# Stick-breaking attention: the keys' remaining shares overwrite the logits in PSUM, and the running product reads them there

## The chip, the cores and the metric

The kernel runs on one core of one Trainium2 chip. The metric is the device time of one execution in microseconds; the figure for a kernel is the median over its runs. The traces are of one profiled execution.

## What is computed

The reference is one layer with two branches that share an input projection: a gated delta rule (a recurrence over chunks of tokens) and stick-breaking attention (8 heads, 64 channels a head, 2048 tokens). Only the attention is touched here. For every query the keys are visited from the latest to the earliest; each takes the share sigmoid(z) of what the later keys have left over.

```python
z = jnp.einsum('bhqd,bhkd->bhqk', q[:, :, q0:end], k[:, :, :end]) * scale
mask = kj < qi
log_keep = jnp.where(mask, jax.nn.log_sigmoid(-z), 0.0)
rest = lax.cumsum(log_keep, axis=3, reverse=True) - log_keep
a = jnp.where(mask, jnp.exp(jax.nn.log_sigmoid(z) + rest), 0.0)
outs.append(jnp.einsum('bhqk,bhkd->bhqd', a, v[:, :, :end]))
```

## The kernel before

The kernel works in stages. The first projects the tokens and prepares the recurrence. Then the attention runs as background work between the matrix products of the last projections (the blocks of the gates): a generator, `attention`, emits the attention's instructions, and the projection calls it after every three products. A clock that the program itself keeps (it adds a cost for each product) decides when a piece is due: `LT`, `LP` and `LZ` are the delays between a tile's logits, its transposes, its products with v, and the next tile. The order of TensorE's instructions is pinned to the order in which they are emitted (`pin`), so TensorE runs the same list whatever the other engines do. The other engines' lists come from a scheduler. After the attention come the recurrence, the up projections and the output projection.

A tile of the attention is 128 queries by 512 keys (128, 256, 384 or 512 on the diagonal), 320 tiles in all, four to a step: 224 of them are 512 wide. The names in the trace for one tile:

- `z`, a bank of PSUM: logits, two products on TensorE (PE). On a diagonal block VectorE (DVE) adds `future`, which masks later keys (L1058; 128 instructions).
- `r` in SBUF: sigmoid of minus the logit, what a key leaves over, written by ScalarE (ACT, L1061); then overwritten in place by VectorE's running product from right to left (the scan, L1065). Its second tensor operand is `zero`, one column broadcast. Column `w` takes the value that the scan starts from (L1064, a copy of one column).
- `s` in SBUF: sigmoid of the logit (ACT, L1062), then multiplied on GpSimd (POOL) by `r` shifted by one column (L1068). These are the weights.
- `carry`: the scan's last value, copied for the tile of earlier keys (DVE, L1067).
- `at`: PE's transposes of `s`, two tiles to a bank (L128); `hi` (ACT, L1083) and `lo` (DVE, L1084) split them into two parts; `av`: PE's products of these with `vt`, summed over all steps of a head in one bank. `att_end` (L1044 on ACT, L1045 on DVE) reads `av` when a head is done; the next head's first product starts another.

`z` has two banks, `at` two, `av` two, `pj` (the projection's sums) two: all eight banks of PSUM. `s` has six buffers, `r` four. `att_pools` and `att_tile` are the functions whose code changes.

Of the kernel before, what the change touches and what calls it, by code (L numbers as in the profile page):

```python
# [18 lines left out]
P = 128  # L19
# [9 lines left out]
SD = 64  # L29
# [8 lines left out]
class Block:  # L38
    """The layer in three stages; DRAM scratch carries what a stage leaves for a later one."""

# [63 lines left out]
    def params(self):  # L104
        """The small parameters."""
        nc, i = self.nc, self.i
        rows = self.a([P, P], "rows")
        nc.gpsimd.memset(rows, 0.0)
        for t, n in ((self.alog, "a_log"), (self.dtb, "dt_bias")):
            self.load(t, i[n].partition_broadcast(P).rearrange("p o n -> p (o n)"))  # L110
        self.load(rows[0:48], i["conv_w"].rearrange("o t (r p) -> (o t r) p", p=P))
        self.load(rows[48:64], i["b_gate"].rearrange("o (r p) -> (o r) p", p=P))
        for k, n in enumerate(("sb_q_gain", "sb_k_gain")):
            for r in range(2):
                self.load(self.gqk[SD * r:SD * r + SD, k:k + 1], i[n].rearrange("o d -> d o"))
        nc.vector.tensor_mul(self.gqk[:, 0:1], self.gqk[:, 0:1], self.gqk[:, 1:2])
        ps = self.pt.tile([P, P], F32, tag="tp", name="tp")
        self.tr(ps, rows, self.ident)
        nc.vector.tensor_copy(self.cols, ps[:, 0:HB])
# [10 lines left out]
    def pin(self, ins):  # L130
        """Keep the tensor engine in program order."""
        if self.chain and self.last is not None:
            self.tc.add_manual_dep(ins.ins, self.last, mybir.DependencyInfo(mybir.DependencyClass.NoSync, mybir.DependencyReason.DATA), reason="order")
        self.last = ins.ins.name if self.chain else None

    def load(self, *args):
        """A load whose queue keeps program order during the first tiles."""
        ins = self.nc.sync.dma_start(*args)
# [5 lines left out]
    def defer(self, steps, fn):  # L144
        """Emit fn after the matrix products of `steps` further steps."""
        self.pending.append((self.now + steps, fn))
# [9 lines left out]
    def advance(self, amount, limit=4.0):  # L156
        """Let the background work emit about `amount` us of the tensor engine's time, or what it has ready."""
        if self.back is None:
# [17 lines left out]
    def drain(self):  # L176
        """All that is left of the background work."""
        while self.back is not None:
            self.advance(1e9)
            self.clock += 0.2  # L180
# [12 lines left out]

    # ---------------------------------------------------------------- stage 1
    def stage1(self):
# [62 lines left out]
    def ready(self, g):  # L258
        """Have the recurrence done for tokens of the up projections' group g."""
        while self.stored < 2 * g + 2:  # L260
# [12 lines left out]
    def gap(self):  # L273
        """Background work between the products of a projection; the recurrence follows the attention."""
        self.advance(self.third)
# [57 lines left out]
    def rsq(self, pool, ssq, n, scale, eps, tag):  # L333
        """(ssq * scale + eps) ** -0.5 on n columns."""
        nc = self.nc
# [6 lines left out]
    def prep_x(self, first):  # L342
        """Normalised x, transposed to channels by tokens, in two parts that f32r products carry exactly."""
        nc = self.nc
# [39 lines left out]
    def mm_chan(self, w, j, tg, between=None):  # L384
        """Projection block [128 channels, 512 tokens]."""
        hi, lo = w
# [9 lines left out]
    def mm_tok(self, w, t, ps, n):  # L396
        """Projection block [128 tokens, n channels]."""
        hi, lo = w
# [30 lines left out]
    def decays(self):  # L429
# [13 lines left out]
        nc.scalar.activation(s2, ab, AF.Sigmoid)  # L443
        # e = exp(-|xa|) = s1 / s2, log1p(e) = 2 atanh(e / (2 + e)), e / (2 + e) = s1 / (2 s2 + s1)
        nc.vector.scalar_tensor_tensor(s2, s2, 2.0, s1, ALU.mult, ALU.add)
# [55 lines left out]
    def qkb_store(self, qn, dst, kind, u, tp):  # L501
        """To channels by tokens, q with both gains, in two parts that f32r products carry exactly."""
        nc = self.nc
# [30 lines left out]
    def conv(self, ps, b, halo):  # L534
        """Causal four-tap convolution of a block; the caller multiplies what it returns for SiLU."""
        nc = self.nc
# [35 lines left out]
    def qk_tok(self, kq, tg, h):  # L572
        """Norms of q and k, k by tokens, and the decay between a chunk's tokens."""
        nc, wk = self.nc, self.wk
# [93 lines left out]

    # gated delta rule: within a chunk of 128 tokens, inverses of the two diagonal blocks of 64
    def dn_solve(self):  # L670
        """Unit triangular inverses by substitution, one block to a partition.

        With b[x, i] = -m[i, x] for x < i, step j adds b[x, j] b[j, i] to b[x, i]."""
        nc, wk = self.nc, self.sv
# [37 lines left out]
    def dn_states(self):  # L712
# [9 lines left out]
        def store(most=0):  # L722
            """Emit what is due, and all but `most` of the rest when its time comes."""
            while tails:
# [54 lines left out]
    def dn_chunk(self, c, loads, st, mo):  # L779
        """One chunk of the recurrence; k and q come without their norms, which nk, nbr and rq carry."""  # L780
        nc = self.nc
# [26 lines left out]
        nc.vector.tensor_tensor(o, ps, o, ALU.add)  # L808
        # rms over a head's values; o carries neither q's norm nor dk ** -0.5 yet
        nc.gpsimd.tensor_tensor(o, o, self.bc(self.rq, c), ALU.mult)  # L810
# [19 lines left out]

    # ---------------------------------------------------------------- stage 2
    def stage2(self):
        """The up projections follow the recurrence; then the rest."""
        NO = S // OG
# [29 lines left out]
    def run_job(self, jobs):  # L864
        """A piece of the first job; the next one's loads run ahead of its end."""
        if jobs:
# [15 lines left out]
    def split(self, src, k, g):  # L882
        """[128, OG] from DRAM in two parts, one of two sets."""
        nc, op = self.nc, self.op
# [17 lines left out]
    def up(self, g):  # L902
        """Gated sum of both up projections for OG tokens, channels by tokens."""
        nc = self.nc
# [34 lines left out]
    def att_pools(self, ctx):  # L939
        nc = self.nc  # L940
        self.ap = ap = ctx.enter_context(self.pool("ap", side="right"))
        self.pz = ctx.enter_context(self.pool("pz", bufs=2, space=PSUM, side="right"))
        self.pa = ctx.enter_context(self.pool("pa", bufs=2, space=PSUM, side="right"))
        self.pv = ctx.enter_context(self.pool("pv", bufs=2, space=PSUM, side="right"))
        self.one = ap.tile([P, 1], F32, name="one", bufs=1)
        self.zero = ap.tile([P, 1], F32, name="zero", bufs=1)
        nc.vector.memset(self.one, 1.0)
        nc.vector.memset(self.zero, 0.0)
        # added to a logit, it makes the key weigh nothing and break nothing
        self.future = ap.tile([P, P], F32, name="future", bufs=1)  # L950
        nc.vector.memset(self.future, -(2.0 ** 100))
        nc.gpsimd.affine_select(self.future, self.future, pattern=[[1, P]], compare_op=ALU.is_ge, fill=0.0, base=0, channel_multiplier=-1)

    # from a tile's products to its transposes, from there to the products with v, between two tiles, in us
    LT, LP, LZ = 4.5, 2.2, 1.3

    def attention(self):
        """Stick-breaking attention: one slot is a tile of 128 queries by 512 keys (or fewer on the diagonal)."""
        nc, ap = self.nc, self.ap
# [4 lines left out]
        def ready():  # L964
            """Emit what is due; the sets of buffers bound how far one kind runs ahead of another."""
            if prods and prods[0][0] <= self.clock:
# [84 lines left out]

    def att_tile(self, qt, kt, i, w, diag, carry):
        nc, ap = self.nc, self.ap
        z = self.pz.tile([P, TG], F32, tag="z", name="z")
# [5 lines left out]
        r = ap.tile([P, TG + 1], F32, tag="r", name="r", bufs=self.NR)  # L1060
        nc.scalar.activation(r[:, :w], z[:, :w], AF.Sigmoid, scale=-(SD ** -0.5))  # L1061
        nc.scalar.activation(s[:, :w], z[:, :w], AF.Sigmoid, scale=SD ** -0.5)  # L1062
        init = self.one if diag else carry[i]
        nc.vector.tensor_copy(r[:, w:w + 1], init)  # L1064
        nc.vector.tensor_tensor_scan(r[:, 0:w][:, ::-1], r[:, 0:w][:, ::-1], self.zero.to_broadcast([P, w]), init, ALU.mult, ALU.add)  # L1065
        carry[i] = ap.tile([P, 1], F32, tag=f"carry{i}", name="carry", bufs=2)
# [4 lines left out]
    def att_trans(self, A, m, edge):  # L1071
        """Two tiles' weights for two blocks of keys, the later block first, keys by queries in two parts."""
        nc, ap = self.nc, self.ap
# [43 lines left out]
```

## Time and profile before

| | us |
|---|---|
| median of 3 runs | 2150.53 |
| lowest and highest of them | 2144.36, 2152.09 |
| the profiled execution: span from first to last instruction | 2144.5 |
| PE busy in it | 2058.2 (96%) |
| DVE, POOL, ACT busy | 1493.9 (70%), 969.8 (45%), 875.2 (41%) |

For the profiled execution the profile gives the span and no other time. The shares are averages over stages with different limits; the attention lies between 794 us and 1589 us of the span, and what an edit to it is worth is read there. PE's matmuls are pipelined, so one that is shown to last 0.39 us may be followed by the next 0.23 us after its start.

### The profile page before, as it was taken

The numbers are of one execution on the slowest core, as the hardware profiler recorded it, in microseconds if no ns is written. First come the engines' busy times: TensorE is split into PE (matmuls) and PEld (weight loads), VectorE is DVE, ScalarE is ACT, GpSimd is POOL, SyncE is SP. The second block draws the span as 40 slices with busy tenths as digits, with TensorE's granted clock in tenths as the row PEclk, the third lists the DMA queues.
The fourth block names the chain that finished last, engine by engine and source line by source line (L and its number), as shares of the span: only waits on it lengthen the run. The fifth ranks groups of instructions, "written<-read, shape, count | busy, mean of one in ns | idle before, by whom it ended". The sixth has DMA issues, their size and how long they took to land.

```text
span 2144.5 us, 36573 instructions
## 1 busy us (share of the span) xinstructions
PE 2058.2 (96%) x12903; PEld 1821.1 (85%) x12903; DVE 1493.9 (70%) x2899; ACT 875.2 (41%) x1695; POOL 969.8 (45%) x820
## 2 busy tenths in 40 slices
PE   7999988999999999999999999999999999999999
PEld 7988767779999988878778888888788899999887
DVE  7367778887998329898889898889854466433221
ACT  6224433422222126666666666666643321211110
POOL 4335666534443215555556655555436655521000
PEclk9999999999999999999999999999999999999999
DMA  7123332226333553333664443333337787764442
GB/s 238 63 62 94 94 104 84 84 73 125 118 114 111 151 137 105 104 113 109 159 171 128 125 117 99 107 103 104 101 107 232 221 272 220 228 183 139 152 136 82
DMA packets 279702, 282.52 MB, mean 132 GB/s; under 512 B 49440, under 2 KB 215520, under 8 KB 279392
## 3 DMA queue, kind: packets, MB, share of 16 engines
q1 hardware_dynamic: 279520, 280.19, 44.8%
q8 instruction: 103, 1.69, 0.3%
q14 instruction: 79, 0.65, 0.1%
HBM read 177.35 MB, written 102.76 MB: 131 GB/s over the span
## 4 chain that ended last, share of the span: by engine, by line
PE 59%; DVE 23%; ACT 6%; DMA 4%; issue 4%; POOL 3%; SPq 0%; ACTq 0%; POOLq 0%; DVEq 0%
PE pj L124 30%; DVE r L1065 9%; PE o L124 8%; PE y L124 6%; DVE acc L548 4%; PE av L124 4%; DVE lo L1084 3%; PE at L128 3%; PE dn L124 3%; PE z L124 3%; ACT r L1061 2%; PE tp L128 1%; DMA wraw<-in_w_in_dram 1%; DVE halo L544 1%; DVE carry L1067 1%
## 5 line engine op out<-in xcount | busy, mean ns | idle before, releaser
L1068 POOL TENSOR_TENSOR s<-s,r 128x512 f32<-128x512 f32 (+2 forms) x320 | 372.5, 1174 | 335.5 <-DVE r L1065 183.7
L124 PE MATMUL pj<-xh,whi 128*128 128x512 f32 x1024 | 420.9, 411 | 12.0 <-ACT u L542 10.1
L124 PE MATMUL pj<-xh,wlo 128*128 128x512 f32 x1024 | 405.3, 396 | 0.0
L124 PE MATMUL pj<-xl,whi 128*128 128x512 f32 x1024 | 404.7, 395 | 0.0
L1065 DVE TENSOR_TENSOR_SCAN r<-r,carry,zero 128x512 f32<-128x512 f32 x192 | 302.2, 1574 | 23.2 <-ACT r L1061 22.0
L124 PE MATMUL pj<-whi,xh 128*128 128x256 f32 (+1 forms) x1024 | 293.3, 286 | 1.0 <-ACT xh L380 1.0
L124 PE MATMUL pj<-whi,xl 128*128 128x256 f32 (+1 forms) x1024 | 289.7, 283 | 0.0
L124 PE MATMUL pj<-wlo,xh 128*128 128x256 f32 (+1 forms) x1024 | 289.5, 283 | 0.2 <-DVE wlo L330 0.2
L124 PEld LDWEIGHTS pj<-xh,whi 128*128 128x128 f32 x1024 | 194.0, 189 | 49.2 <-ACT u L542 14.9
L1061 ACT ACTIVATE r<-z 128x512 f32<-128x512 f32 (+2 forms) x320 | 171.9, 537 | 152.2 <-PE z L124 53.9
L124 PEld LDWEIGHTS pj<-xh,wlo 128*128 128x128 f32 x1024 | 193.3, 189 | 44.5
L124 PEld LDWEIGHTS pj<-xl,whi 128*128 128x128 f32 x1024 | 194.3, 190 | 32.0
L1084 DVE TENSOR_TENSOR lo<-at,hi 128x512 fp32r<-128x512 f32 (+1 forms) x288 | 183.7, 653 | 28.3 <-ACT hi L1083 27.1
L124 PEld LDWEIGHTS pj<-whi,xh 128*128 128x128 f32 x1024 | 194.1, 190 | 1.4 <-ACT xh L380 1.4
L124 PEld LDWEIGHTS pj<-wlo,xh 128*128 128x128 f32 x1024 | 194.3, 190 | 0.5 <-DVE wlo L330 0.5
L124 PEld LDWEIGHTS pj<-whi,xl 128*128 128x128 f32 x1024 | 193.9, 189 | 0.3 <-DVE xl L381 0.3
L1083 ACT CAST hi<-at 128x512 fp32r<-128x512 f32 (+1 forms) x288 | 154.3, 571 | 96.7 <-PE at L128 94.7
L124 PE MATMUL z<-kt,qt 128*128 128x512 f32 (+3 forms) x640 | 189.4, 377 | 4.2 <-ACT s L1062 2.9
L330 POOL TENSOR_TENSOR wlo<-wraw,whi 128x512 fp32r<-128x512 f32 (+2 forms) x66 | 122.4, 1854 | 112.6 <-ACT whi L329 111.7
L1062 ACT ACTIVATE s<-z 128x512 f32<-128x512 f32 (+2 forms) x320 | 171.1, 535 | 0.0
L128 PE MATMUL at<-ident,s 128*128 128x128 f32 x1088 | 156.9, 274 | 11.3 <-POOL s L1068 11.1
L124 PE MATMUL av<-lo,vt 128*128 128x256 f32 x576 | 148.4, 292 | 17.0 <-DVE r L1064 9.9
(200 smaller groups left out, 4293.5 us busy)
## 6 DMA issues: line engine op xcount, KB each, us to landing
kt<-d_k SPq DMA_DIRECT2D x160, 128.0 KB, 3.0
vt<-d_v SPq DMA_DIRECT2D x80, 256.0 KB, 3.5
xt<-in_x_dram SPq DMA_DIRECT2D x32, 512.0 KB, 3.9
qt<-d_q SPq DMA_DIRECT2D x64, 256.0 KB, 5.2
d_g<-sg SPq DMA_DIRECT2D x128, 128.0 KB, 2.5
gt<-d_g SPq DMA_DIRECT2D x64, 256.0 KB, 3.6
wraw<-in_w_in_dram SPq DMA_DIRECT2D x56, 256.0 KB, 3.2
wraw<-in_w_in_dram SPq DMA_DIRECT2D x18, 512.0 KB, 3.8
```

The source lines that it names most:

```text
L124: self.pin(self.nc.tensor.matmul(out, lhsT, rhs, **kw))
L128: self.pin(self.nc.tensor.transpose(*args))
L330: (eng or nc.gpsimd).tensor_tensor(lo[:, ks, :n], raw[:, :, :n], hi[:, ks, :n].bitcast(F32), ALU.subtract)
L544: nc.vector.tensor_copy(halo, u[:, TG:TG + 3])
L548: nc.vector.scalar_tensor_tensor(acc, u[:, k:k + TG], self.tap(k, b), acc, ALU.mult, ALU.add)
L1061: nc.scalar.activation(r[:, :w], z[:, :w], AF.Sigmoid, scale=-(SD ** -0.5))
L1062: nc.scalar.activation(s[:, :w], z[:, :w], AF.Sigmoid, scale=SD ** -0.5)
L1065: nc.vector.tensor_tensor_scan(r[:, 0:w][:, ::-1], r[:, 0:w][:, ::-1], self.zero.to_broadcast([P, w]), init, ALU.mult, ALU.add)
L1067: nc.vector.tensor_copy(carry[i], r[:, 0:1])
L1068: nc.gpsimd.tensor_mul(s[:, :w], s[:, :w], r[:, 1:w + 1])
L1083: nc.scalar.copy(hi[:, c:], flat[:, c:])
L1084: nc.vector.tensor_tensor(lo[:, c:], flat[:, c:], hi[:, c:].bitcast(F32), ALU.subtract)
```

## The change

ScalarE now writes `s` first, and then overwrites the logits with the remaining shares in the same bank of PSUM. The scan reads them from there and writes `r` in SBUF. The copy of the start value into `r` moves from VectorE to GpSimd. The logits get three banks in place of two, and the value sums `av` one in place of two. (Comments that the change also removes are left out of the diff.)

```diff
@@ att_pools
-        self.pz = ctx.enter_context(self.pool("pz", bufs=2, space=PSUM, side="right"))
+        self.pz = ctx.enter_context(self.pool("pz", bufs=3, space=PSUM, side="right"))
         self.pa = ctx.enter_context(self.pool("pa", bufs=2, space=PSUM, side="right"))
-        self.pv = ctx.enter_context(self.pool("pv", bufs=2, space=PSUM, side="right"))
+        self.pv = ctx.enter_context(self.pool("pv", bufs=1, space=PSUM, side="right"))
@@ att_tile
         r = ap.tile([P, TG + 1], F32, tag="r", name="r", bufs=self.NR)
-        nc.scalar.activation(r[:, :w], z[:, :w], AF.Sigmoid, scale=-(SD ** -0.5))
         nc.scalar.activation(s[:, :w], z[:, :w], AF.Sigmoid, scale=SD ** -0.5)
+        nc.scalar.activation(z[:, :w], z[:, :w], AF.Sigmoid, scale=-(SD ** -0.5))
         init = self.one if diag else carry[i]
-        nc.vector.tensor_copy(r[:, w:w + 1], init)
-        nc.vector.tensor_tensor_scan(r[:, 0:w][:, ::-1], r[:, 0:w][:, ::-1], self.zero.to_broadcast([P, w]), init, ALU.mult, ALU.add)
+        nc.vector.tensor_tensor_scan(r[:, 0:w][:, ::-1], z[:, 0:w][:, ::-1], self.zero.to_broadcast([P, w]), init, ALU.mult, ALU.add)
+        nc.gpsimd.tensor_copy(r[:, w:w + 1], init)
         carry[i] = ap.tile([P, 1], F32, tag=f"carry{i}", name="carry", bufs=2)
         nc.vector.tensor_copy(carry[i], r[:, 0:1])
         nc.gpsimd.tensor_mul(s[:, :w], s[:, :w], r[:, 1:w + 1])
```

PE's list of instructions is the same in both kernels. VectorE's list, at a place in the first third of the attention, before (the scan has the name SCALAR_TENSOR_TENSOR here):

```order
L1065 SCALAR_TENSOR_TENSOR r<-r,carry,zero 128x512
L1064 COPY r<-carry 128x1
L1067 COPY carry<-r 128x1
L1065 SCALAR_TENSOR_TENSOR r<-r,carry,zero 128x512
L1067 COPY carry<-r 128x1
L1084 TENSOR_TENSOR lo<-at,hi 128x512 x2
L1064 COPY r<-carry 128x1
L1065 SCALAR_TENSOR_TENSOR r<-r,carry,zero 128x512
L1067 COPY carry<-r 128x1
L1084 TENSOR_TENSOR lo<-at,hi 128x512 x2
```

and at the same place now:

```order
L1068 SCALAR_TENSOR_TENSOR r<-z,carry,zero 128x512
L1071 COPY carry<-r 128x1
L1068 SCALAR_TENSOR_TENSOR r<-z,carry,zero 128x512
L1071 COPY carry<-r 128x1
L1088 TENSOR_TENSOR lo<-at,hi 128x512 x2
L1068 SCALAR_TENSOR_TENSOR r<-z,carry,zero 128x512
L1071 COPY carry<-r 128x1
L1088 TENSOR_TENSOR lo<-at,hi 128x512 x2
```

The copies into `r` are gone from VectorE, the scan reads `z`, and the order of the rest stays. GpSimd's list at the start of the attention, before:

```order
L952 AFFINE_SELECT future<-future 128x128
L330 TENSOR_TENSOR wlo<-wraw,whi 128x512
L1068 TENSOR_TENSOR s<-s,r 128x128
L1068 TENSOR_TENSOR s<-s,r 128x256
L1068 TENSOR_TENSOR s<-s,r 128x384
```

and now (L1072 is what was L1068):

```order
L952 AFFINE_SELECT future<-future 128x128
L330 TENSOR_TENSOR wlo<-wraw,whi 128x512
L1069 COPY r<-one 128x1
L1072 TENSOR_TENSOR s<-s,r 128x128
L1069 COPY r<-one 128x1
L1072 TENSOR_TENSOR s<-s,r 128x256
L1069 COPY r<-one 128x1
L1072 TENSOR_TENSOR s<-s,r 128x384
```

A copy of one column now stands among the multiplications. One such copy stands ahead of these rows, so a tile's copy comes a multiplication early.

## Rows read from the trace of the kernel before

**Rows 1.** The page's first line.

```profile
span 2144.5 us, 36573 instructions
```

**Rows 2.** Attention's stretch: busy us (instructions) of PE, PEld, DVE, ACT, POOL; clock, DMA.

```profile
794.00:1589.00 795.00, 762.28 (x4422) 648.90 (x4421) 698.66 (x1420) 517.74 (x1058) 442.75 (x368) 1.00 0.42 114
```

**Rows 3.** Waits of PE, the same stretch: us in total, times, longest.

```profile
PE at L128 <- POOL s L1068: 11.1, 16, 1.5
PE av L124 <- DVE r L1064: 9.9, 14, 1.5
PE av L124 <- DVE lo L1084: 5.8, 10, 1.4
PE z L124 <- ACT s L1062: 2.9, 8, 0.7
```

**Rows 4.** Timeline of DVE, 930 to 943 us: start, length, what.

```profile
931.77 1.28 DVE L1065 TENSOR_TENSOR_SCAN r<-r,carry,zero 128x512 f32<-128x512 f32 x1
...
933.31 2.08 DVE L1065 TENSOR_TENSOR_SCAN r<-r,carry,zero 128x512 f32<-128x512 f32 x1
...
937.90 2.18 DVE L1065 TENSOR_TENSOR_SCAN r<-r,carry,zero 128x512 f32<-128x512 f32 x1
...
940.18 0.68 DVE L1084 TENSOR_TENSOR lo<-at,hi 128x512 fp32r<-128x512 f32 x1
```

**Rows 5.** Timeline of POOL, the same stretch.

```profile
933.22 1.09 POOL L1068 TENSOR_TENSOR s<-s,r 128x512 f32<-128x512 f32 x1 [3.27 <-DVE r L1064]
```

**Rows 6.** Timeline of PE, 930 to 944 us.

```profile
931.96 0.62 PE L124 MATMUL z<-kt,qt 128*128 128x512 f32 x2
932.42 0.39 PE L124 MATMUL pj<-xh,whi 128*128 128x512 f32 x1
...
937.48 0.62 PE L124 MATMUL z<-kt,qt 128*128 128x512 f32 x2
...
940.91 0.39 PE L124 MATMUL av<-lo,vt 128*128 128x256 f32 x1 [1.32 <-DVE r L1064]
```

**Rows 7.** Instructions by line: count, shortest/median/longest in ns.

```profile
L1065 DVE TENSOR_TENSOR_SCAN r<-r,carry,zero x192: 1265/1358/2418, 803.2 to 1580.2; 128x512 f32<-128x512 f32 x192
...
L1084 DVE TENSOR_TENSOR lo<-at,hi x288: 525/681/694, 805.2 to 1586.1; 128x512 fp32r<-128x512 f32 x112, 128x384 fp32r<-128x384 f32 x32
...
L1068 POOL TENSOR_TENSOR s<-s,r x320: 407/1092/2555, 796.4 to 1582.4; 128x512 f32<-128x512 f32 x96, 128x128 f32<-128x128 f32 x32, 128x384 f32<-128x384 f32 x32
```

**Rows 8.** Groups by line and shape: busy us, mean ns, idle before.

```profile
L1065 DVE TENSOR_TENSOR_SCAN r<-r,carry,zero 128x512 f32<-128x512 f32 x192 | 302.2, 1574 | 23.2 <-ACT r L1061 22.0
...
L1064 DVE COPY r<-carry 128x1 f32<-128x1 f32 x192 | 26.7, 140 | 0.2
...
L1064 DVE COPY r<-one 128x1 f32<-128x1 f32 x128 | 17.1, 140 | 0.1
...
L1068 POOL TENSOR_TENSOR s<-s,r 128x512 f32<-128x512 f32 x224 | 300.2, 1350 | 257.1 <-DVE r L1065 123.3 <-DVE r L1064 40.6 <-ACT s L1062 26.1
```

**Rows 9.** The same view: DVE reading SBUF and PSUM; ACT's sigmoid; a small POOL instruction.

```profile
L490 DVE TENSOR_REDUCE ss<-sq 128x8 f32<-128x512 f32 x32 | 21.7, 679 | 7.1 <-ACT sq L488 7.0
...
L588 DVE COPY tk<-tp 128x512 f32<-128x512 f32 x16 | 10.9, 681 | 0.0
...
L1061 ACT ACTIVATE r<-z 128x512 f32<-128x512 f32 x224 | 134.8, 602 | 91.1 <-PE z L124 53.9 <-POOL s L1068 14.6 <-DVE r L1064 8.0
...
L339 POOL TENSOR_TENSOR rxr<-rxv,mhalf 128x1 f32<-128x1 f32 x16 | 9.3, 583 | 19.4 <-DVE rxv L338 19.3
```

**Rows 10.** Timeline: first and last of 31 handovers of `av` between heads.

```profile
831.64 0.67 DVE L1045 TENSOR_TENSOR ot<-av,tmp 64x512 f32<-64x512 f32 x1
...
834.02 0.28 PE L124 MATMUL av<-hi,vt 128*128 128x256 f32 x1
...
1551.24 0.68 DVE L1045 TENSOR_TENSOR ot<-av,tmp 64x512 f32<-64x512 f32 x1
...
1551.46 0.39 PE L124 MATMUL av<-hi,vt 128*128 128x256 f32 x1
```

## The prediction

> **What bounds the kernel now.** I read the page's first line for the span, 2144.5 us [rows 1], then cut out the stretch that the edit touches. Between 794 and 1589 us PE is busy for 762.3 of 795 us; DVE for 698.7 (88%), ACT for 517.7 (65%), POOL for 442.8 (56%) [rows 2]. PE's list is pinned and the same in both kernels, so the change can only shorten or lengthen PE's waits: 795.0 - 762.3 = 32.7 us of idle time. The list of PE's waits says for whom [rows 3]: 11.1 us for the weights from POOL, 9.9 + 5.8 = 15.7 us ahead of the products with v, for which DVE is late, and 2.9 us for a bank of logits; 29.7 us in 48 waits.
>
> A little more is hidden. Two products for logits are shown to last 0.62 us, yet the next product starts 0.46 us after them [rows 6]: a wait up to 0.16 us shows as busy time. Over 48 waits that is up to 48 x 0.16 = 7.7 us, so the whole prize is some 40 us.
>
> Why is DVE late? The scan of 512 keys lasts from 1.27 to 2.42 us, with a median of 1.36 [rows 7]: the same work, so something holds it up. The timeline shows what. At 931.77 a scan runs in 1.28 us, and the next row of POOL starts only after it. At 933.22 POOL starts a multiplication of 1.09 us, at 933.31 the scan starts, and it takes 2.08 us; the last of three such scans takes 2.18 [rows 4, 5]. `lo` stands behind these scans in DVE's list, starts at 940.18, and PE waits 1.32 us for it at 940.91 [rows 4, 6]. POOL suffers likewise when the scan is first: its multiplications have a median of 1.09 us and reach 2.56 [rows 7].
>
> `lo` is the row to hold beside it: it reads one operand from PSUM and one from SBUF, runs among the same multiplications, and its 288 instructions never take more than 0.69 us, for a median of 0.68 [rows 7]. Now the scan reads `r` and `zero`, both in SBUF; after the change it reads PSUM and `zero`, as `lo` does.
>
> [...]
>
> **The change part by part.**
> *The scan reads PSUM.* Held up no longer, the 192 scans with a carry take 192 x 1.28 = 245.8 us in place of 302.2 [rows 4, 8]: 56.4 us less on DVE. The 128 scans on the diagonal gain too; I leave them out. No row has a scan from PSUM. From below it takes 1.27 us, the shortest now; from above 1.57, today's mean, if nothing is relieved. The nearest rows to a price of PSUM are a pass of 512 columns from SBUF, 679 ns, and one from PSUM, 681 ns [rows 9]. I take 1.28.
>
> [...]
>
> *The copy of the start value.* DVE loses 26.7 + 17.1 = 43.8 us [rows 8]. With the scans that leaves 698.7 - 56.4 - 43.8 = 598.5 us, 75% of the stretch.
>
> *POOL.* Its 224 wide multiplications go from 300.2 us to 224 x 1.09 = 244.2, 56.0 less [rows 7, 8]. It gains 320 copies of one column. From below a copy costs nothing that matters; from above 0.58 us, a power of one column [rows 9]. From the shortest multiplication, 0.407 us (128 columns), and the median, 1.092 (512), a straight line gives 1.78 ns a column and 0.18 us at one column: I take that, nearest in kind, 320 x 0.18 = 58 us. POOL stays at 445 us; with the upper price it would be 573 (72%). A tile's copy stands a multiplication early in POOL's list, so it runs while POOL waits for the scan; if that cover is gone, it delays the weights by 0.18 us a tile.
>
> *ACT.* It has the same two sigmoids, but the scan now waits for the second, so a tile's chain is longer by at most one sigmoid, 0.60 us [rows 9]. No row writes a sigmoid to PSUM; from 0 to 0.1 us either way on 320 of them is at most 32 us in ACT's 277 idle us. A chain that was held up loses 0.8 us on the scan and up to 1.0 on the multiplication, so it ends sooner; one that ran free ends up to 0.6 us later.
>
> *Three banks of logits.* A bank is now held until its scan ends. The logits of 931.96 are scanned from 933.31 to 935.39 (one of the held-up scans), and the third next product for logits comes at 937.48 [rows 4, 6]: 2.1 us to spare. I charge 0.5 us in all.
>
> *One value bank.* A head's first product with v must now wait until `att_end` has read the sums of the head before. At the first of 31 handovers DVE ends at 832.31 and PE comes at 834.02: 1.7 us to spare. At the last it ends at 1551.92 and PE would have come at 1551.46: 0.46 us late [rows 10], the worst of all; one more is late by less. I charge 2 us, since DVE's order has shifted a little.
>
> *The sum.* Ahead of the products with v: the three scans shown lose some 2.5 us, which is more than the 1.32 us that PE waited, so I take back 13 of 15.7. For the weights: 6 of 11.1, since free chains pay for the second sigmoid. For logits: 2 of 2.9. That is 21 of 29.7 us; of the hidden 7.7 the same share is 5.4. Together 26.4, less 2.5 for the banks: 24 us. The profiled span would be 2144.5 - 24 = 2120.5. It lies near the lowest of the three runs (2144.4), and the metric is their median, 2150.5; I take the saving off that: 2126.5, say **2126 us**.
>
> **The rivals.**
> *A. The relief doesn't come.* The scan keeps an SBUF operand, the broadcast `zero`; if that collides with POOL all the same, only the copies leave DVE. Each of the 48 waits then has some three copies of 0.14 us less ahead of it [rows 8], and half of that reaches PE: 48 x 0.2 = 10 us, less 2.5 for the banks and some 3 for longer chains: 2146. Against it: `lo` has an SBUF operand too, and is never stretched [rows 7]. To this I count that the relief comes and PE finds other waits.
>
> *B. All of it.* Every wait and the hidden part go: 32.7 + 7.7 = 40 us, 2110. For it: DVE gets 25% idle time. Against: the longer chain of the free tiles.
>
> *C. Slower, by the single value bank.* If ACT and DVE read a head's sums late by some 2.5 us more than now, because those reads stand behind scans in lists made anew, PE waits about 1.5 us at each of 31 handovers: 47 us, against the 24 gained, 2150.5 + 23 = 2173. It decides from 24 / 31 = 0.8 us a handover upward. For it: the spare time is under 2 us at both ends of the list [rows 10]. Against: DVE's list gets lighter, not heavier.
>
> **How the numbers follow.** My forecast has 0.63 (its own range 2115 to 2137), A 0.20, B 0.08, C 0.09. A reaches from 2139 to 2155 with the spread of the runs (2144 to 2152). The range runs from 2107, B with the lowest run's lead, to 2146, the middle of A: outside are C, somewhat under half of A, and a little below, together near 0.2. Within 0.5% (10.8 us, about what a measurement of this kernel tells from no change) means 2139.7 to 2161.3: A's upper part and a little of C, 0.15. Faster: the forecast, B and the rest of A, 0.77. Slower: 0.08.
>
> **What would show it.** In the profile after: scans of 512 near 1.28 us with longest and median together; multiplications near 1.09 with none over 1.5; no copy of the start value on DVE; DVE near 600 us in the stretch; PE's waits ahead of the products with v near 3 us, for the weights near 5. A scan from PSUM at 1.5 us or more, a copy on POOL over 0.6, or waits of the first product with v behind L1045 over 10 us in all would make the prediction wrong.

## The result, and the profile after

The changed kernel takes 2125.39 us (median of 4 runs, 2121.59 to 2129.35), the kernel before 2148.62 us with one more run counted in. The ratio is 0.9895, with a 95% interval from 0.9879 to 0.9911: 23 us faster. The profiled execution has a span of 2124.2 us, 20.3 less than [rows 1]; its own time is 2125.88, so some 1.7 us lie around the span.

The attention now ends near 1568 us. Its stretch (columns as in [rows 2]):

```profile
794.00:1568.00 774.00, 758.23 (x4418) 650.95 (x4418) 613.52 (x1100) 520.45 (x1057) 406.10 (x687) 1.00 0.43 117
```

The stretch is 21 us shorter, and PE is idle for 774.0 - 758.2 = 15.8 us of it, against 32.7. VectorE is busy for 613.5 us (79%), GpSimd for 406.1. PE's waits from 794 to 1589 us, which answer to [rows 3]:

```profile
PE av L124 <- ACT hi L1087: 4.6, 4, 2.3
PE av L124 <- DVE lo L1088: 4.4, 11, 1.1
PE av L124 <- DVE carry L1071: 3.8, 7, 1.1
PE at L128 <- POOL s L1072: 1.4, 6, 0.5
```

The scan and the multiplication by line (shortest/median/longest in ns), which answer to [rows 7]:

```profile
L1068 DVE TENSOR_TENSOR_SCAN r<-z,carry,zero x192: 1264/1282/1286, 802.2 to 1559.5; 128x512 f32<-128x512 f32 x192
...
L1072 POOL TENSOR_TENSOR s<-s,r x320: 406/1092/1114, 795.8 to 1560.9; 128x512 f32<-128x512 f32 x96, 128x128 f32<-128x128 f32 x32, 128x384 f32<-128x384 f32 x32
```

No scan and no multiplication is held up any more: the longest scan is 1.29 us where it was 2.42, the longest multiplication 1.11 where it was 2.56. The groups by shape answer to [rows 8 and 9]:

```profile
L1068 DVE TENSOR_TENSOR_SCAN r<-z,carry,zero 128x512 f32<-128x512 f32 x192 | 245.8, 1280 | 65.7 <-ACT z L1066 60.3 <-POOL r L1069 2.3 <-POOL s L1072 1.4
...
L1072 POOL TENSOR_TENSOR s<-s,r 128x512 f32<-128x512 f32 x224 | 245.0, 1094 | 257.5 <-DVE r L1068 257.2 <-PE pj L124 0.2
...
L1069 POOL COPY r<-carry 128x1 f32<-128x1 f32 x192 | 35.4, 184 | 0.0
...
L1066 ACT ACTIVATE z<-z 128x512 f32<-128x512 f32 x224 | 134.1, 599 | 0.0
```

The scan from PSUM costs what the undisturbed one from SBUF cost, 1.28 us ([rows 4], at 931.77). The copy on GpSimd takes 184 ns, and a sigmoid written to PSUM 599 ns (602 to SBUF). VectorE now waits for the second sigmoid: 60.3 us ahead of the wide scans, where it waited 22.0 us for the first in [rows 8].

Two of PE's new waits can be read in the timeline. The longest, on ScalarE and then PE:

```profile
1289.13 0.62 ACT L329 CAST whi<-wraw 128x512 fp32r<-128x512 f32 x1 [3.69 <-DMA wraw<-in_w_in_dram]
1289.65 0.58 ACT L1087 CAST hi<-at 128x512 fp32r<-128x512 f32 x1
...
1290.28 0.38 PE L124 MATMUL av<-hi,vt 128*128 128x256 f32 x1 [2.32 <-ACT hi L1087]
```

A cast of projection weights waits 3.7 us for its transfer, `hi` stands behind it in ScalarE's list, and PE behind `hi`. PE waits so at three places, 3.6 us of the 4.6 above (1.05 us at 1042.58, 2.32 here, 0.25 at 1433.05). At the first two TensorE's granted clock falls to 0.50 soon after, for 3.4 us each time (columns as in [rows 2]):

```profile
1043.10:1046.50 3.40, 3.32 (x12) 3.04 (x13) 3.12 (x9) 2.50 (x7) 2.17 (x6) 0.50 0.92 211
...
1292.30:1295.70 3.40, 3.40 (x12) 2.72 (x11) 3.37 (x7) 2.68 (x5) 2.45 (x4) 0.50 0.50 152
```

In them the projection's products of 512 columns start 0.42 to 0.43 us apart, where they start some 0.23 us apart at a clock of 1.00 (from 1292.65 and from 1430.54 on). From that each stretch costs about half its length, together some 3.4 us (an estimate), and they count as busy time. In the trace of the kernel before, the clock is 1.00 all the way from 794 to 1589 us. That the waits brought it down is not shown: there a wait of 1.49 us at 1306.35 has no fall behind it.

The other wait stands at the last handover between heads, on VectorE and PE:

```profile
1530.59 0.66 DVE L1045 TENSOR_TENSOR ot<-av,tmp 64x512 f32<-64x512 f32 x1
...
1531.35 0.36 PE L124 MATMUL av<-hi,vt 128*128 128x256 f32 x1 [1.03 <-ACT hi L1087]
```

The wait is put down to `hi`, but that `hi` had ended at 1530.41; what ends at 1531.25 is VectorE's read of the last head's sums. This is the single value bank at work: 1.0 us here, the rest of the 4.6 for `hi`, and 0.3 us at one other handover, at 977.69.

### The profile page after: what moved, and what is told of

Read it like the earlier page. It is cut to its first block, busy times and chain, and to the rows that moved or that the text cites. A ratio compares the mean times of both kernels' runs of the same rounds, so it can differ in the third digit from the quotient of the medians.

```text
span 2124.2 us, 36554 instructions
## 1 busy us (share of the span) xinstructions
PE 2057.2 (97%) x12903; PEld 1826.7 (86%) x12903; DVE 1408.6 (66%) x2579; ACT 878.0 (41%) x1695; POOL 932.3 (44%) x1140
## 4 chain that ended last, share of the span: by engine, by line
PE 37%; DVE 5%; DMA 4%; ACT 2%; issue 2%; POOL 1%; SPq 0%; DVEq 0%; ACTq 0%; POOLq 0%
PE pj L124 9%; PE o L124 8%; PE y L124 7%; PE dn L124 4%; PE av L124 3%; PE at L128 3%; DVE r L1068 2%; PE z L124 2%; DMA wraw<-in_w_in_dram 2%; DVE lo L1088 1%; ACT z L1066 1%; ACT s L1065 1%; DMA raw<-in_w_out_dram 0%; POOL xl L880 0%; DMA raw<-in_w_up_a_dram 0%
## 5 line engine op out<-in xcount | busy, mean ns | idle before, releaser
L1072 POOL TENSOR_TENSOR s<-s,r 128x512 f32<-128x512 f32 (+2 forms) x320 | 306.1, 957 | 336.8 <-DVE r L1068 330.6
L1068 DVE TENSOR_TENSOR_SCAN r<-z,carry,zero 128x512 f32<-128x512 f32 x192 | 245.8, 1280 | 65.7 <-ACT z L1066 60.3
L330 POOL TENSOR_TENSOR wlo<-wraw,whi 128x512 fp32r<-128x512 f32 (+2 forms) x66 | 116.5, 1765 | 129.6 <-ACT whi L329 127.4
L1066 ACT ACTIVATE z<-z 128x512 f32<-128x512 f32 (+2 forms) x320 | 170.8, 534 | 0.1
L548 DVE SCALAR_TENSOR_TENSOR acc<-u,cols,acc 128x512 f32<-128x512 f32 x144 | 154.6, 1073 | 5.0
```

Of the source, the lines that this page charges most:

```text
L330: (eng or nc.gpsimd).tensor_tensor(lo[:, ks, :n], raw[:, :, :n], hi[:, ks, :n].bitcast(F32), ALU.subtract)
L548: nc.vector.scalar_tensor_tensor(acc, u[:, k:k + TG], self.tap(k, b), acc, ALU.mult, ALU.add)
L1066: nc.scalar.activation(z[:, :w], z[:, :w], AF.Sigmoid, scale=-(SD ** -0.5))
L1068: nc.vector.tensor_tensor_scan(r[:, 0:w][:, ::-1], z[:, 0:w][:, ::-1], self.zero.to_broadcast([P, w]), init, ALU.mult, ALU.add)
L1072: nc.gpsimd.tensor_mul(s[:, :w], s[:, :w], r[:, 1:w + 1])
```

## The experiments

Three theories were set against each other. Theory 1, that of the prediction: the scan and GpSimd's multiplications held each other up because both of the scan's operands lay in SBUF, and the gain is the relief. Theory 2: the gain is the third bank of logits. Theory 3: the gain is the copies that leave VectorE. Medians and ratios are against runs of the kernel before on the same chip (2147.8 us in the first four experiments, 2146.9 in the others).

| | us | ratio, 95% interval |
|---|---|---|
| banks only | 2148.7 | 1.0003 (0.999 to 1.0016) |
| copies on GpSimd only | 2141.1 | 0.9962 (0.9949 to 0.9976) |
| scan from PSUM, copies on VectorE | 2124.8 | 0.9895 (0.987 to 0.992) |
| zeros in PSUM, scan from SBUF | 2113.9 | 0.9837 (0.9819 to 0.9854) |
| the change with two and two banks | 2138.9 | 0.9956 (0.9939 to 0.9972) |
| the change with three copies a tile | 2124.8 | 0.9892 (0.9876 to 0.9908) |
| zeros in PSUM, sigmoids swapped | 2117.9 | 0.9864 (0.9845 to 0.9883) |
| zeros in PSUM, copies on GpSimd | 2107.3 | 0.9807 (0.9787 to 0.9827) |

**Banks only.** The kernel before with the new bank counts:

```diff
-        self.pz = ctx.enter_context(self.pool("pz", bufs=2, space=PSUM, side="right"))
+        self.pz = ctx.enter_context(self.pool("pz", bufs=3, space=PSUM, side="right"))
-        self.pv = ctx.enter_context(self.pool("pv", bufs=2, space=PSUM, side="right"))
+        self.pv = ctx.enter_context(self.pool("pv", bufs=1, space=PSUM, side="right"))
```

> The kernel before, with three banks of logits and one value bank and nothing else. Theory 1 (the scan was held up by GpSimd because both its operands lay in SBUF; the gain is the relief): scans stay at a mean near 1.55 us for 512 keys, PE's 2.9 us of waits for a bank of logits go, the value bank costs up to 2 us: no change, ratio 0.998 to 1.002, some 2148 us. Theory 2 (the gain is the third bank of logits): most of it is here, 2130 us or less, ratio 0.991. Theory 3 (the gain is the copies that leave VectorE): no change.

It took 2148.7 us: no change, and theory 2 falls. Its scans still reach 2.42 us.

**Copies only.** The kernel before with the copy on GpSimd:

```diff
-        nc.vector.tensor_copy(r[:, w:w + 1], init)
         nc.vector.tensor_tensor_scan(r[:, 0:w][:, ::-1], r[:, 0:w][:, ::-1], ...)
+        nc.gpsimd.tensor_copy(r[:, w:w + 1], init)
```

> The kernel before, with the copy of the start value on GpSimd (behind the scan in the program) and nothing else; the scan still reads SBUF. Theory 1: scans still have a mean near 1.55 us and reach over 2; VectorE loses 44 us of copies, which gives a part alone: 2136 to 2146 us, ratio 0.994 to 0.999. Theory 3: most of the gain is here, 2128 us or less, ratio 0.990. Theory 2: no change.

2141.1 us, 6.7 us less: a part, as theory 1 has it. Scans by line and GpSimd's copies by group:

```profile
L1064 DVE TENSOR_TENSOR_SCAN r<-r,carry,zero x192: 1266/1284/2306, 802.8 to 1575.0; 128x512 f32<-128x512 f32 x192
```

```profile
L1065 POOL COPY r<-carry 128x1 f32<-128x1 f32 x192 | 110.2, 582 | 0.0
```

Scans still reach 2.31 us, and the same copy of one column, whose median is 186 ns, reaches 1232 and takes 582 on average, where the changed kernel shows 184: it too is held up while the scan has both operands in SBUF.

**Scan from PSUM, copies on VectorE.** The changed kernel with that one line back:

```diff
-        nc.gpsimd.tensor_copy(r[:, w:w + 1], init)
+        nc.vector.tensor_copy(r[:, w:w + 1], init)
```

> The changed kernel, with the copy of the start value back on VectorE; the scan reads the shares from PSUM, the banks are three and one. Theory 1: scans of 512 keys at 1.28 us, shortest and longest within 0.03; VectorE has the 44 us of copies again; two thirds of the gain or more: 2126 to 2134 us, ratio 0.990 to 0.994. Theory 3: the gain is gone, 2142 us or more, ratio over 0.997.

2124.8 us, the time of the changed kernel and a little better than theory 1 had it (2126 to 2134). The whole gain is there without moving the copies, and theory 3 falls for this change.

**Zeros in PSUM.** The kernel before, the scan untouched in SBUF, only its second operand, one column of zeros, in the bank that a single value bank leaves free:

```diff
-        self.pv = ctx.enter_context(self.pool("pv", bufs=2, space=PSUM, side="right"))
+        self.pv = ctx.enter_context(self.pool("pv", bufs=1, space=PSUM, side="right"))
-        self.zero = ap.tile([P, 1], F32, name="zero", bufs=1)
+        self.zero = ctx.enter_context(self.pool("pzero", bufs=1, space=PSUM, side="right")).tile([P, 1], F32, name="zero", bufs=1)
```

> The kernel before, with the column of zeros, the scan's second operand, in PSUM; the scan still reads and writes r in SBUF in place, the copies stay on VectorE, logits have two banks and the values one (its other bank holds the zeros). Theory 1, where what matters is that no more than one operand of the scan lies in SBUF: scans of 512 keys at 1.28 to 1.35 us with no long ones, multiplications on GpSimd at 1.09, and as much of the gain as the run with the copies back on VectorE shows: 2126 to 2136 us, ratio 0.990 to 0.995. If the hold-up comes from the scan's reading and writing the same tile in SBUF, whatever its second operand: scans stay at a mean near 1.55 and the time near 2149, ratio 0.998 to 1.002.

2113.9 us, faster than expected and 11 us faster than the changed kernel. Its scans by line and PE's waits:

```profile
L1065 DVE TENSOR_TENSOR_SCAN r<-r,carry,zero x192: 1260/1273/1284, 803.1 to 1547.1; 128x512 f32<-128x512 f32 x192
```

```profile
PE z L124 <- ACT s L1062: 5.1, 7, 1.6
PE av L124 <- DVE lo L1084: 1.9, 5, 0.5
PE av L124 <- DVE r L1064: 0.7, 3, 0.3
PE av L124 <- DVE carry L1067: 0.4, 2, 0.2
```

This is the cleanest test of theory 1: one column moved to PSUM, and with it every long scan is gone, though the scan reads and writes `r` in SBUF as before. (One value bank in place of two, which goes with it, changed nothing in the run with the banks only.) What mattered in these runs is that no more than one of the scan's two tensor operands lies in SBUF: with the other in PSUM the longest scan is 1.28 us here and 1.29 in the changed kernel, with both in SBUF 2.31 to 2.42. That it beats the change says that the change pays for its own way to the same relief: waits ahead of the products with v are 3.0 us here, 12.8 in the changed kernel; for a bank of logits they are 5.1 here and 0.2 there. All of PE's waits are 8.4 us here and 15.0 there: 6.6 us of the 13.9 by which the two profiled spans differ. The mean granted clock of the profiled execution is 0.998 here and 0.994 there, where the two falls cost some 3.4 us (the estimate above).

**Two and two banks.** The changed kernel with the bank counts of before:

```diff
-        self.pz = ctx.enter_context(self.pool("pz", bufs=3, space=PSUM, side="right"))
+        self.pz = ctx.enter_context(self.pool("pz", bufs=2, space=PSUM, side="right"))
-        self.pv = ctx.enter_context(self.pool("pv", bufs=1, space=PSUM, side="right"))
+        self.pv = ctx.enter_context(self.pool("pv", bufs=2, space=PSUM, side="right"))
```

> The changed kernel with two banks of logits and two value banks, as before the change; the scan reads the shares in PSUM, the copy is on GpSimd. If the third bank is needed once a bank is held until its scan ends: PE waits for a bank of logits in many of the 320 tiles (in the trace of before, a scan ended after the second next product for logits had begun for 63 tiles, 37 us in all, held-up scans included), so some 20 to 35 us of new waits: 2140 to 2155 us, ratio 0.996 to 1.003. If bank counts don't matter: 2125 us, ratio 0.989, and no such waits.

2138.9 us, just under the range expected if the third bank is needed: 13.5 us of the gain are lost. PE's first wait names it:

```profile
PE z L124 <- DVE r L1068: 21.9, 30, 2.1
```

Once a bank is held until its scan ends, the third bank is needed; without the held bank it was worth nothing. (Two value banks came back with it; the single one cost 1.3 us.)

**Three copies a tile.** The changed kernel with the copy on GpSimd issued three times:

```diff
         nc.gpsimd.tensor_copy(r[:, w:w + 1], init)
+        nc.gpsimd.tensor_copy(r[:, w:w + 1], init)
+        nc.gpsimd.tensor_copy(r[:, w:w + 1], init)
```

> The changed kernel with the copy of the start value issued three times on GpSimd, 640 copies more of 0.18 us, 117 us more work there. If the copies run while GpSimd waits for the scan (cover as I took it): within 3 us of the changed kernel, 2123 to 2129 us. If they lie on the path of the weights: 0.37 us a tile, of which the pairs that PE waits for show some 10 to 20 us: 2135 us or more.

2124.8 us, no change: the copies do run while GpSimd waits for the scan.

**Zeros in PSUM, sigmoids swapped.** The run with the zeros in PSUM, with ScalarE's two sigmoids in the order of the change, to see what the longer chain costs:

```diff
-        nc.scalar.activation(r[:, :w], z[:, :w], AF.Sigmoid, scale=-(SD ** -0.5))
         nc.scalar.activation(s[:, :w], z[:, :w], AF.Sigmoid, scale=SD ** -0.5)
+        nc.scalar.activation(r[:, :w], z[:, :w], AF.Sigmoid, scale=-(SD ** -0.5))
```

> The run with the zeros in PSUM, with ScalarE's two sigmoids in the order of the change (the weights' first), so that the scan waits for the second of them. That run took 2113.9 us, the changed kernel 2125.4; they differ by the order of the sigmoids, by the bank that holds the scan's operand, by bank counts and by which engine copies. If the longer chain (0.5 to 0.6 us a tile) makes the difference: 2120 to 2127 us, with PE's waits ahead of the products with v back near 10 us. If not: 2112 to 2117 us.

2117.9 us, 4 us more than without the swap, just above the one answer and below the other. The runs overlap (2112.2 to 2115.8 us without the swap, 2114.1 to 2120.2 with it), so the size is rough. PE's waits for the products with v come up from 3.0 us to some 9, and those for a bank of logits go down from 5.1 to 0.3:

```profile
PE av L124 <- ACT hi L1083: 2.7, 3, 1.7
PE av L124 <- DVE lo L1084: 2.5, 7, 0.7
PE av L124 <- DVE carry L1067: 1.8, 5, 0.6
PE av L124 <- DVE r L1064: 1.5, 4, 0.5
...
PE z L124 <- ACT r L1062: 0.3, 1, 0.3
```

The swap has changed more than the length of the chain. At three places one `hi` now stands behind a cast of projection weights that waits for its transfer, as in the changed kernel; all of the 2.7 us for `hi` are there. Without the swap both `hi` stand ahead of these casts, and two of the three, with one more, hold up the sigmoids that free a bank of logits: 3.7 of the 5.1 us. So the swap is a part, some 4 of the 11 us by which the change stands behind the zeros in PSUM; how much of that is the longer chain and how much ScalarE's order is not shown.

**Zeros in PSUM, copies on GpSimd.** The two together, against the run with the zeros in PSUM:

```diff
-        nc.vector.tensor_copy(r[:, w:w + 1], init)
         nc.vector.tensor_tensor_scan(r[:, 0:w][:, ::-1], r[:, 0:w][:, ::-1], ...)
+        nc.gpsimd.tensor_copy(r[:, w:w + 1], init)
```

> The run with the zeros in PSUM, with the copy of the start value moved to GpSimd too. If VectorE is no longer what PE waits for once the scans are 1.28 us: 2111 to 2116 us, no gain over 2113.9, as the changed kernel with its copies back on VectorE (2124.8) took the time of the changed kernel. If the copies still count: 2104 to 2110 us.

2107.3 us, the fastest of all: 39.6 us under the kernel before, 18 under the changed one. The copies do count here, the second of the two answers. Stretch and PE's first waits:

```profile
794.00:1549.00 755.00, 747.94 (x4414) 647.96 (x4413) 616.97 (x1100) 516.59 (x1056) 405.21 (x687) 1.00 0.43 120
```

```profile
PE z L124 <- ACT s L1062: 3.2, 5, 1.6
PE av L124 <- DVE lo L1084: 2.2, 7, 0.5
```

PE's idle time in the stretch is down to 7.1 us.

## Why the prediction was right, step by step

**The time.** Forecast 2126, measured 2125.4; a saving of 24 us from the median against 23.2. On the profiled span the saving is 20.3 us against the 24 that the sum gave. That the total fits is in part luck: terms of the sum were off by up to 10 us and nearly cancel.

**The scan reads PSUM.** Right, and the cause shown. 192 scans were to take 245.8 us and take 245.8; no price of PSUM shows: the mean is 1280 ns from PSUM, and the undisturbed scan from SBUF was 1.28 us. No scan is over 1.29 us with the shares in PSUM (the changed kernel, its copies on VectorE, three copies a tile) or with the zeros there (copies on either engine); with both operands in SBUF they reach 2.3 to 2.4.

**The copies and POOL.** The price of a copy, put at 0.18 us from a line through two shapes, is 0.184. The cover is shown: two more copies a tile change nothing (2124.8 us). Their worth on VectorE depends on what else is late: 6.7 us off the kernel before, nothing on top of the scan from PSUM, 6.6 us on top of the zeros in PSUM. With the scan from PSUM VectorE waits for the second sigmoid anyway; that this is why its copies cost nothing there is read from the waits, not shown by a run.

**ACT.** Right that a sigmoid written to PSUM costs no more (599 ns, 602 to SBUF). That the scan must wait for the second sigmoid was priced as a delay of the free chains, in the 5.1 us of waits for the weights that the sum left standing. The size is about right, since the swap alone puts some 4 us on the time, but the place is wrong: 1.4 us are left at the weights, and the waits stand ahead of the products with v.

**The banks.** With three banks PE waits 0.2 us for a bank of logits (0.5 was charged); the run with two shows what the third holds off, 21.9 us of waits and 13.5 us of time. The single value bank makes PE wait 1.3 us at two handovers (2 were charged). Rival C, the value bank as the new bound, is refuted.

**The sum's terms.** The total is right, but two terms were mis-sized in opposite directions. For the weights I took back 6 of 11.1 us; 9.7 came back, since the multiplications lost their long ones and no wait over 0.5 us is left. By [rows 7] a held-up multiplication could lose 2.56 - 1.09 = 1.47 us, and not the 1.0 that I put down. Ahead of the products with v I took back 13 of 15.7; only some 3 came back, and 12.8 us of waits are left. The failed step there was to take one place, the three stretched scans shown, for all the waits. The waits for VectorE (`r`, `lo` and `carry`) fell by 8, from 16.2 us to 8.2, and 4.4 us of new waits for `hi` came on top (4.6 in place of 0.2): 3.6 behind casts that wait for a transfer, 1.0 for the single value bank. The second sigmoid, for which VectorE waits 60.3 us, makes the scans later too, but how much of the 8.2 it is stays open. The sum has no term for the casts, and none for the clock that fell twice, some 3.4 us. Idle time fell by 16.9 us; the rest of the 20.3, 3.4 us, is what the hidden part gave back (5.4 was taken) less what the clock took.

**The rivals.** A (the relief doesn't come) is refuted by the longest scan; its side remark, that PE would find other waits, is half true: 4.6 us for `hi`. B (all waits go) is closer to the run with zeros in PSUM and copies on GpSimd, 2107, than to this change.

**Open.** Between the swapped run with its zeros in PSUM (2117.9) and the changed kernel with its copies on VectorE (2124.8) 7 us remain. They differ in where each operand of the scan lies, in how long a bank of logits is held, and in the number of these banks. The waits ahead of the products with v are larger in the latter (13.0 us against some 9), but no run tells which difference makes them.

## What to carry to other kernels

When one instruction's longest time is far above its shortest for the same shape, look at what runs on the other engine at that moment: here VectorE and GpSimd held each other up (scans of up to 2.42 us, multiplications of up to 2.56), and moving one operand of VectorE's instruction to PSUM freed both (up to 1.28 and 1.11 us with the zeros there). Move the operand that costs least to move: a constant column in PSUM gave the whole relief (2113.9 us), while moving the data lengthened the chain and took a bank for longer (2125.4). When a bank is held longer, count its banks again in the same edit. And when two instructions change places, read the whole list of their engine again: here a third one came to stand behind a cast that waits for a transfer.

## What the runs showed of the hardware

An operand of a single column, broadcast along the scan, is enough for the hold-up: with it in SBUF beside `r` scans reached 2.42 us, with it in PSUM and `r` in SBUF none was over 1.29. GpSimd's small copies are held up as well: 582 ns on average beside scans with both operands in SBUF, 184 ns beside scans with one.

In the trace of the kernel before, a multiplication beside a long scan keeps its 1.09 us. The one of 933.22 ends at 934.31, and the scan that starts at 933.31 ends at 935.39, 1.08 us later. A scan that starts together with a multiplication (the scan is the one of 937.90 in [rows 4]) ends 1.09 us after it:

```profile
937.90 1.09 POOL L1068 TENSOR_TENSOR s<-s,r 128x512 f32<-128x512 f32 x1 [1.25 <-DVE r L1065]
```

So each of these two scans takes what is left of the multiplication and then some 1.08 us, where an undisturbed one takes 1.28. How the hardware brings that about is not shown.
